# Another order for the matmuls of the down product, and another start for its rows

## The chip, the cores and the metric

The kernel runs on one core of one Trainium2 chip. The metric is the time of one execution on the device in microseconds, median of several runs. A profile is one further execution with every instruction's start and length recorded; its span runs from the first instruction to the last.

## The reference

One layer of a hybrid decoder, in float32, for 256 prompt tokens and 8 x 8 sample tokens (320 tokens, width 2048), that share the weights:

```
z = rms_norm(x) @ w_in                       # B, C, h, q, k, v and two gates
y_conv = (B * conv3(C * h)) @ w_conv_out
y_attn = window_attention(q, k, v) @ w_attn_out
h = x + (sigmoid(g_c) * y_conv + sigmoid(g_a) * y_attn) @ w_o
a = silu(rms_norm(h) @ w_gate) * (rms_norm(h) @ w_up)      # 5632 features
y = rms_norm(h + a @ w_down)
```

The change lies in the last product, `a @ w_down`, which contracts 5632 features into 2048 columns. Everything is returned in float32, with the new key, value and convolution states.

## The kernel before

**Two parts of every number.** TensorE multiplies operands of type `float32r`. Weights and activations are therefore each split into a high part, which `float32r` holds, and the small remainder, the low part. A product is the sum of three: high weight times high activation, high weight times low activation, low weight times high activation. ScalarE makes the high part of a tile of weights (`whi`, line 128), VectorE the low part (`wlo`, line 129), from a raw tile (`wraw`) that SyncE loads 512 KB at a time. The pools hold four raw tiles, three high ones and three low ones. In most products the weights are stationary, and a matmul moves the 320 columns of one part of the activations past them (`product`, line 161).

**The down product.** The 5632 features are 44 slices of 128, taken in two halves of 28 and 16 slices (`FH`). After the gate and up products of a half, `down(half, c0)` (line 930) makes 512 columns of the output at a time, that is four chunks `c` of 128 columns, one PSUM tile `ps[c]` each: four such blocks in the first half, three in the second. The last block of the second half is written out apart at the end (lines 1077 to 1116). Weights come two slices `k` at a time (a set); the last four slices of a block make one larger set. For a slice and a chunk there are up to three matmuls:

- m = 0, line 954: the high weights are stationary and 512 columns move. Of these, 320 are the high parts of all tokens and 192 the low parts of all tokens but the first 128.
- m = 1, line 958, for chunk 0 alone: the low parts of the first 128 tokens are stationary and the 512 columns of the high weights move, once for all four chunks, into a tile of its own (`dl`, or `rowacc` in the last block). This one moves weights.
- m = 2, line 962: the low weights are stationary and the 320 high columns move.

In the last block lines 1106 and 1111 are m = 0 and m = 2; there 384 columns move in m = 0, m = 1 is missing from the loop, and line 1146 brings what is left with the activations stationary and the weights moving.

**The order.** `passes(order, end)` (line 149) puts the matmuls of a set in order: m = 0 of a pair (k, c), with m = 1 behind it, then the next pair; m = 2 comes three pairs late (`LAG`). In the last set of a block, `end`, one chunk is finished before the next begins, and in the first and the last set the pairs are sorted by chunk. The chunks are sorted there because the same four PSUM tiles serve the next block: three additions on VectorE (lines 973 to 975) empty each of them into the residual.

The order of instructions on an engine is that of the text as far as the instructions' inputs are ready by the reckoning of the program that builds the kernel; it moves later work ahead of an instruction that it takes to be waiting.

**The rows.** `a_rows` (line 909) lays the activations of a half into one tile of `float32r`. Each row, 64 elements per slice and part, is read in eight streams, 4 elements from each in turn (`placed` and `turns`, lines 96 and 100). The streams lie 912 elements apart in the first half and 528 in the second; both are 16 more than a multiple of 128. `LEAD_F` elements stand ahead of the rows, and `LEAD_L` between them and the low rows of m = 1. In the program as built, a partition's high and low weights lie at byte 39040 and multiples of 4096 behind it, the activations' tile at byte 144160. Counted modulo 128 elements (512 bytes) the weights begin at 32, the rows at 112, 48 short of the weights, and the low rows of m = 1 at 32 like the weights. In the last block some of the converted weights are kept in the rest of the activations' tile (`free`), at 32 too, and some in the tile `more` at byte 96000, which is at 64, that is 32 elements further.

Of the kernel before, what the change touches and what calls it, by code (L numbers as in the profile page):

```python
# [43 lines left out]
JR = P // NP  # L44
JM = 2 * JT - JR
XB = [1] * 4 + [2] * 6
LEAD_X, LEAD_C, LEAD_A, LEAD_M, LEAD_F, LEAD_L = 16, 8, 8, 24, 40, 48
TOK = [(0, 128), (128, 128), (256, 64)]


# [1 line left out]
def hybrid_layer(ctx: ExitStack, tc: tile.TileContext, a: dict, o: list):  # L52
# [15 lines left out]
    def ps_acc(name):  # L68
        return acc.tile([P, 512], F32, tag="acc", name=name)

    def ps_aux(name):
        return aux[0].tile([P, 512], F32, tag="aux", name=name)
# [3 lines left out]
    def u(s):  # L76
        uid[0] += 1
        return f"{s}_{uid[0]}"

    def after(*marks):  # L80

        es = ExitStack()
        for m in marks:
            es.enter_context(tc.issue_after(m.ins))
        return es
# [10 lines left out]
    def placed(ap):  # L96

        return ap.rearrange("p (s j) -> p s j", s=NP)

    def turns(ap):  # L100

        return ap.rearrange("p s (i b) -> p i s b", b=4)
# [24 lines left out]
    def split_to(hi, lo, src):  # L127
        last["hi"] = nc.scalar.activation(hi, src, AF.Copy)  # L128
        last["lo"] = nc.vector.tensor_sub(lo, src, hi.bitcast(F32))  # L129
# [19 lines left out]
    def passes(order, end):  # L149

        seq, low = [], []
        for k, c in order:
            if end and low and low[-1][1] != c:
                seq, low = seq + low, []
            seq += [(k, c, 0), (k, c, 1)]
            low.append((k, c, 2))
            if len(low) > LAG:
                seq.append(low.pop(0))
        return seq + low

    def product(load, nk, xh, xl, name, tiles=None, loaded=None):

        ps = [ps_acc(u(name)) for _ in range(2)]
        k0 = 0
        for n in tiles or [min(KT, nk - k) for k in range(0, nk, KT)]:
            hi, lo = load(k0, n)
            if loaded:
                loaded()
            order = [(k, c) for k in range(n) for c in range(2)]
            if k0 + n == nk:  # L170
                order.sort(key=lambda kc: kc[1])
            for k, c, i in passes(order, k0 + n == nk):
                kc = k0 + k
                w, x = ((hi, xh), (hi, xl), (lo, xh))[i]
                last["mm"] = nc.tensor.matmul(  # L175
                    turns(fives(ps[c][:, :T])), w[:, k, c * P:(c + 1) * P], turns(x(kc)),
                    start=(kc == 0 and i == 0), stop=(kc == nk - 1 and i == 2),
                )
            k0 += n
            while pending:  # L180
                with after(last["lo"], last["mm"]):
                    pending.pop(0)()
            tick()
        return ps
# [147 lines left out]
    def kv_product(tiles, x_after):  # L332
# [4 lines left out]
        for i, n in enumerate(tiles):  # L337
            hi, lo = load_kv(k0, n)
            if i == 0:
                x_prep(1)  # L340
            for b in x_after.get(i, ()):
                x_load(b)
            order = [(k, c) for k in range(n) for c in range(4)]
            if k0 + n == KC:
                order.sort(key=lambda kc: kc[1])
            seq = passes(order, k0 + n == KC)
            if i == 0:
                seq.sort(key=lambda kcm: kcm[2])
            for k, c, m in seq:
                kc = k0 + k  # L350
                if k0 and (k, c, m) == (0, 3 if n > 1 else 1, 0) and k0 + n < KC:
                    for kk in range(tiles[i + 1]):
                        x_prep(k0 + n + kk)
                    tick()
                w, x = ((hi, xh), (hi, xl), (lo, xh))[m]
                last["mm"] = nc.tensor.matmul(  # L356
                    turns(fives(ps[c][:, :T])), w[:, k, c * P:(c + 1) * P], turns(x(kc)),
                    start=(kc == 0 and m == 0), stop=(kc == KC - 1 and m == 2),
                )
            k0 += n  # L360
            if i == 0:
                tick()
# [507 lines left out]
    for mp in range(8):  # L870
# [5 lines left out]
        for c in range(2):  # L876
            k = mp * 2 + c
# [49 lines left out]
    def h_parts(k):  # L927
        return parts_of(hT[:, k, :])

    def down(half, c0):  # L930

        nf, f0 = FH[half], half * FH[0]
        ps = [ps_acc(u("dn")) for _ in range(4)]
        low = ps_aux(u("dl")) if c0 < E0 else rowacc
        sets = [[k] for k in range(0, nf, 2)]
        sets[-2:] = [sets[-2] + sets[-1]]
        for i, k0s in enumerate(sets):
            parts = {}
            for k0 in k0s:
                raw = wp.tile([P, 2, 512], F32, tag="wraw", name=u("wraw"), bufs=4)  # L940
                nc.sync.dma_start(raw, w_d[c0 // 512, :, f0 + k0:f0 + k0 + 2, :])
                hi = wp.tile([P, 2, 512], F32R, tag="whi", name=u("whi"), bufs=3)
                lo = wp.tile([P, 2, 512], F32R, tag="wlo", name=u("wlo"), bufs=3)
                split_to(hi, lo, raw)
                for j in range(2):
                    parts[k0 + j] = (hi[:, j, :], lo[:, j, :])
            end = i == len(sets) - 1
            order = [(k, c) for k in parts for c in range(4)]
            if end or i == 0:
                order.sort(key=lambda kc: kc[1])  # L950
            for k, c, m in passes(order, end):
                cs = slice(c * P, (c + 1) * P)
                if m == 0:
                    nc.tensor.matmul(  # L954
                        turns(placed(ps[c])), parts[k][0][:, cs], turns(a_move(k)), start=k == 0, stop=False
                    )
                elif m == 1 and c == 0:
                    nc.tensor.matmul(  # L958
                        low, a_low(k), parts[k][0], start=k == 0, stop=k == nf - 1 and c0 < E0
                    )  # L960
                elif m == 2:
                    last["mm"] = nc.tensor.matmul(  # L962
                        turns(placed(ps[c])[:, :, 0:JT]), parts[k][1][:, cs], turns(a_move(k)[:, :, 0:JT]),
                        start=False, stop=k == nf - 1,
                    )
            if pending and i % 2 == 1:
                with after(last["lo"], last["mm"]):
                    pending.pop(0)()
        mark["out"] = []
        for c in range(4):  # L970
            k = c0 // P + c
            got, (first, rest) = placed(ps[c]), h_parts(k)
            nc.vector.tensor_add(first, first, got[:, :, 0:JR])
            nc.vector.tensor_add(rest, rest, got[:, :, JR:JT])
            mark["out"].append(nc.vector.tensor_add(rest, rest, got[:, :, JT:]))
        if c0 < E0:
            ys = ylow[:, c0:c0 + 512]
            if half == 0:
                nc.scalar.activation(ys, low, AF.Copy)
            else:  # L980
                nc.vector.tensor_add(ys, low, ys)

    for half in range(2):
# [86 lines left out]
        for c0 in range(0, D if half == 0 else E0, 512):  # L1070
            down(half, c0)
            if half == 1:
                pending.append(lambda c0=c0: rows_of(c0))
                pending.append(lambda c0=c0: rest_of(range(c0 // P, c0 // P + 4)))
# [23 lines left out]
    for i, ks in enumerate(sets):  # L1098
        end = i == len(sets) - 1
        order = [(k, c) for k in ks for c in range(4)]  # L1100
        if end or i == 0:
            order.sort(key=lambda kc: kc[1])
        for k, c, m in passes(order, end):
            cs = slice(c * P, (c + 1) * P)
            if m == 0:
                nc.tensor.matmul(  # L1106
                    turns(placed(ps[c])[:, :, JR:]), held[k][0][:, cs], turns(a_move(k)[:, :, JR:]),
                    start=k == 0, stop=k == nf - 1,
                )
            elif m == 2:  # L1110
                last["mm"] = nc.tensor.matmul(
                    turns(placed(ps[c])[:, :, 0:JT]), held[k][1][:, cs], turns(a_move(k)[:, :, 0:JT]),
                    start=False, stop=k == nf - 1, skip_group_check=True,
                )
        if pending and i % 2 == 1:
            with after(last["lo"], last["mm"]):
                pending.pop(0)()
# [5 lines left out]
    for c in range(4):  # L1123
        k = E0 // P + c
# [11 lines left out]
    for c in (2, 3):  # L1136
        k = E0 // P + c
# [118 lines left out]
```

## Time and profile before

| | |
|---|---|
| median of 3 runs | 1603.67 us (1603.61 to 1603.93) |
| profiled execution | 1604.88 us |
| its span | 1603.1 us |
| TensorE (PE) busy | 99% of the span |
| VectorE (DVE), ScalarE (ACT) busy | 55%, 41% |
| granted TensorE clock | 0.998 |

Busy times are of the span. In a timeline a row is a run of like instructions: start in us, length in us, engine, line, operation, tiles, shape and count. Matmuls overlap in it, since the length runs to the modelled end; what a matmul costs is the distance from its start to the next one's.

### The profile page before, as it was taken

To read this page: it belongs to the slowest core of one execution; us is meant where nothing else is said; L and a number is where in the kernel's file an instruction comes from. 1 tells how busy PE (TensorE), PEld (TensorE's weight loads), DVE (VectorE), ACT (ScalarE), POOL (GpSimd) and SP (SyncE) were. 2 spreads that over 40 slices of the span, in tenths; PEclk is the share of its full clock that TensorE was granted. 3 is DMA by queue.
4 is the path that set the end of the run, shared out by engine and by line. 5 is a ranking of instruction groups with operands and counts; after the bars stand their busy time and mean duration, and the time that the engine had idled before them with its cause. 6 is when DMAs were issued, how large, how long until landed. Compare 5 with 4: busy or idle time off the path is not lost.

```text
span 1603.1 us, 26407 instructions
## 1 busy us (share of the span) xinstructions
PE 1593.3 (99%) x10955; PEld 1555.5 (97%) x10955; DVE 885.6 (55%) x1316; ACT 651.5 (41%) x928; POOL 78.3 (5%) x123
## 2 busy tenths in 40 slices
PE   9999999999999999999999999999999999999998
PEld 9999999999999999999999999998888999999887
DVE  7879555555554445556555555553444455555556
ACT  7545343433333334444333333333333334344443
POOL 1101311000000003320000000000000000000000
PEclk9999999999999999999999999999999999999999
DMA  7554546544444444444444444444444444444552
GB/s 268 170 167 149 184 135 195 170 158 158 158 158 158 158 158 158 155 154 155 157 158 158 158 158 158 158 158 155 154 155 156 156 158 158 158 158 158 181 174 93
DMA packets 74400, 258.14 MB, mean 161 GB/s; under 512 B 8552, under 2 KB 11928, under 8 KB 74152
## 3 DMA queue, kind: packets, MB, share of 16 engines
q1 hardware_dynamic: 71880, 249.86, 47.5%
q0 software_dynamic: 1968, 5.90, 1.3%
q8 instruction: 86, 1.41, 0.4%
q10 hardware_dynamic: 432, 0.69, 0.1%
q14 instruction: 34, 0.28, 0.0%
HBM read 253.30 MB, written 5.08 MB: 161 GB/s over the span
## 4 chain that ended last, share of the span: by engine, by line
PE 98%; DVE 1%; DMA 1%; ACT 0%; issue 0%; DVEq 0%; SPq 0%; ACTq 0%
PE fu L175 18%; PE fg L175 18%; PE dn L954 9%; PE ga L175 7%; PE gc L175 7%; PE wo L175 7%; PE dn L962 6%; PE B L175 3%; PE C L175 3%; PE H L175 3%; PE ya L175 3%; PE yc L175 3%; PE q L175 3%; PE dl L958 2%; PE kv L356 1%; PE dn L1106 1%
## 5 line engine op out<-in xcount | busy, mean ns | idle before, releaser
L129 DVE TENSOR_TENSOR wlo<-wraw,whi 128x1024 fp32r<-128x1024 f32 (+1 forms) x461 | 562.1, 1220 | 590.5 <-ACT whi L128 582.1
L128 ACT ACTIVATE whi<-wraw 128x1024 fp32r<-128x1024 f32 (+1 forms) x461 | 485.6, 1055 | 718.8 <-PE dn L954 144.7
L954 PE MATMUL dn<-a_t,whi 128*128 128x512 f32 x640 | 211.0, 385 | 0.0
L175 PE MATMUL fu<-hh_t,whi 128*128 128x320 f32 x704 | 205.1, 301 | 0.0
L175 PE MATMUL fg<-hh_t,whi 128*128 128x320 f32 x704 | 205.1, 301 | 0.0
L175 PE MATMUL fu<-hl_t,whi 128*128 128x320 f32 x704 | 205.1, 301 | 0.0
L175 PE MATMUL fg<-hl_t,whi 128*128 128x320 f32 x704 | 205.1, 301 | 0.0
L175 PE MATMUL fu<-hh_t,wlo 128*128 128x320 f32 x704 | 158.8, 301 | 0.0
L175 PE MATMUL fg<-hh_t,wlo 128*128 128x320 f32 x704 | 158.8, 301 | 0.0
L962 PE MATMUL dn<-a_t,wlo 128*128 128x320 f32 x640 | 146.7, 302 | 0.0
L954 PEld LDWEIGHTS dn<-a_t,whi 128*128 128x128 f32 x640 | 118.6, 187 | 19.4
L175 PEld LDWEIGHTS fu<-hh_t,whi 128*128 128x128 f32 x704 | 131.7, 187 | 0.0
L175 PEld LDWEIGHTS fu<-hl_t,whi 128*128 128x128 f32 x704 | 131.7, 187 | 0.0
L175 PEld LDWEIGHTS fg<-hl_t,whi 128*128 128x128 f32 x704 | 131.7, 187 | 0.0
L175 PEld LDWEIGHTS fg<-hh_t,whi 128*128 128x128 f32 x704 | 131.7, 187 | 0.0
L962 PEld LDWEIGHTS dn<-a_t,wlo 128*128 128x128 f32 x640 | 111.1, 188 | 9.3
L175 PEld LDWEIGHTS fu<-hh_t,wlo 128*128 128x128 f32 x704 | 116.2, 187 | 0.0
L175 PEld LDWEIGHTS fg<-hh_t,wlo 128*128 128x128 f32 x704 | 116.2, 187 | 0.0
L175 PE MATMUL gc<-xh_t,whi 128*128 128x320 f32 x256 | 74.5, 301 | 0.0
L175 PE MATMUL gc<-xl_t,whi 128*128 128x320 f32 x256 | 74.5, 301 | 0.0
L175 PE MATMUL ga<-xh_t,whi 128*128 128x320 f32 x256 | 74.5, 301 | 0.0
L175 PE MATMUL ga<-xl_t,whi 128*128 128x320 f32 x256 | 74.5, 301 | 0.0
(309 smaller groups left out, 2676.4 us busy)
## 6 DMA issues: line engine op xcount, KB each, us to landing
wraw<-in_w_in_dram SPq DMA_DIRECT2D x128, 512.0 KB, 3.8
wraw<-in_w_gate_dram SPq DMA_DIRECT2D x88, 512.0 KB, 3.7
wraw<-in_w_up_dram SPq DMA_DIRECT2D x88, 512.0 KB, 3.6
wraw<-in_w_down_dram SPq DMA_DIRECT2D x88, 512.0 KB, 3.4
wraw<-in_w_o_dram SPq DMA_DIRECT2D x32, 512.0 KB, 3.7
wraw<-in_w_conv_out_dram SPq DMA_DIRECT2D x16, 512.0 KB, 3.6
wraw<-in_w_attn_out_dram SPq DMA_DIRECT2D x16, 512.0 KB, 3.6
wraw<-in_w_kv_dram SPq DMA_DIRECT2D x6, 512.0 KB, 6.7
```

The source lines that it names most:

```text
L128: last["hi"] = nc.scalar.activation(hi, src, AF.Copy)
L129: last["lo"] = nc.vector.tensor_sub(lo, src, hi.bitcast(F32))
L175: last["mm"] = nc.tensor.matmul(turns(fives(ps[c][:, :T])), w[:, k, c * P:(c + 1) * P], turns(x(kc)), start=(kc == 0 and i == 0), stop=(kc ...
L356: last["mm"] = nc.tensor.matmul(turns(fives(ps[c][:, :T])), w[:, k, c * P:(c + 1) * P], turns(x(kc)), start=(kc == 0 and m == 0), stop=(kc ...
L954: nc.tensor.matmul(turns(placed(ps[c])), parts[k][0][:, cs], turns(a_move(k)), start=k == 0, stop=False)
L958: nc.tensor.matmul(low, a_low(k), parts[k][0], start=k == 0, stop=k == nf - 1 and c0 < E0)
L962: last["mm"] = nc.tensor.matmul(turns(placed(ps[c])[:, :, 0:JT]), parts[k][1][:, cs], turns(a_move(k)[:, :, 0:JT]), start=False, stop=k == ...
L1106: nc.tensor.matmul(turns(placed(ps[c])[:, :, JR:]), held[k][0][:, cs], turns(a_move(k)[:, :, JR:]), start=k == 0, stop=k == nf - 1,)
```

## The change

A new function puts the matmuls of a set in turn: all m = 0 of the set (eight of them, two slices by four chunks), then m = 1 of both slices, then all eight m = 2. Where `end` is set, this is done chunk by chunk. It replaces `passes` in the down product (line 951) and in the last block (line 1103); the other products keep `passes`. `LEAD_F` goes from 40 to 52 and `LEAD_L` from 48 to 36: the rows begin 12 elements later, and the low rows of m = 1, and what lies behind them, stay where they were.

```
-LEAD_X, LEAD_C, LEAD_A, LEAD_M, LEAD_F, LEAD_L = 16, 8, 8, 24, 40, 48
+LEAD_X, LEAD_C, LEAD_A, LEAD_M, LEAD_F, LEAD_L = 16, 8, 8, 24, 52, 36
...
+    def in_turn(order, end):
+
+        groups = [[kc for kc in order if kc[1] == c] for c in range(4)] if end else [order]
+        return [(k, c, m) for g in groups for m in range(3) for k, c in g]
...
-            for k, c, m in passes(order, end):
+            for k, c, m in in_turn(order, end):
...
-        for k, c, m in passes(order, end):
+        for k, c, m in in_turn(order, end):
```

## The prediction

> **What bounds the kernel now.** I read the page first (busy shares, the chain that ended last, the costliest groups), then the busy times of the down product's stretch, then its timeline matmul by matmul.
>
> ```profile
> span 1603.1 us, 26407 instructions
> PE 1593.3 (99%) x10955; PEld 1555.5 (97%) x10955; DVE 885.6 (55%) x1316; ACT 651.5 (41%) x928; POOL 78.3 (5%) x123
> PE 98%; DVE 1%; DMA 1%; ACT 0%; issue 0%; DVEq 0%; SPq 0%; ACTq 0%
> L954 PE MATMUL dn<-a_t,whi 128*128 128x512 f32 x640 | 211.0, 385 | 0.0
> L962 PE MATMUL dn<-a_t,wlo 128*128 128x320 f32 x640 | 146.7, 302 | 0.0
> ```
>
> TensorE (PE) is busy for 99% of the span and holds 98% of the chain; the two big groups of the down product have no idle time ahead of them (the last number of their rows). Nothing that another engine or a queue does is late in this stage. The row of the first half's down product, with stretch and length, then the busy time of PE, PEld, DVE, ACT and POOL, the granted clock, the DMA share and GB/s, says the same:
>
> ```profile
> 1081.00:1269.70 188.70, 188.70 (x1011) 167.76 (x1010) 81.17 (x104) 60.93 (x62) 0.00 (x0) 1.00 0.50 156
> ```
>
> TensorE works through all 188.70 us at a granted clock of 1.00. So the change, which neither adds nor removes a matmul, can move the time in two ways only: the distance from one matmul's start to the next one's changes, or TensorE begins to wait. It touches this stretch, the second half's three blocks and the last block.
>
> One set of two slices in the first half, from its first m = 0 to that of the next:
>
> ```profile
> 1151.58 0.38 PE L954 MATMUL dn<-a_t,whi 128*128 128x512 f32 x1
> 1151.81 0.39 PE L958 MATMUL dl<-whi,a_t 128*128 128x512 f32 x1
> 1152.04 0.83 PE L954 MATMUL dn<-a_t,whi 128*128 128x512 f32 x3
> 1152.71 0.31 PE L962 MATMUL dn<-a_t,wlo 128*128 128x320 f32 x1
> 1152.85 0.38 PE L954 MATMUL dn<-a_t,whi 128*128 128x512 f32 x1
> 1153.07 0.39 PE L958 MATMUL dl<-whi,a_t 128*128 128x512 f32 x1
> 1153.31 0.30 PE L962 MATMUL dn<-a_t,wlo 128*128 128x320 f32 x1
> 1153.44 0.38 PE L954 MATMUL dn<-a_t,whi 128*128 128x512 f32 x1
> ...
> 1154.39 0.72 PE L962 MATMUL dn<-a_t,wlo 128*128 128x320 f32 x4
> 1154.94 0.38 PE L954 MATMUL dn<-a_t,whi 128*128 128x512 f32 x1
> ```
>
> A set takes 1154.94 - 1151.58 = 3.36 us. Three m = 0 in a row take 0.67, so 0.223 each; the m = 1 that moves weights 0.23 to 0.24; four m = 2 in a row 0.55, so 0.138 each. The program has 80 sets of this size: 14 in each of four blocks and 8 in each of three, with the last four slices of a block counted as two. Of these, 59 are neither first nor last in a block (11 x 4 + 5 x 3), and they alone get a really different order. The last block has eight more, with shorter matmuls.
>
> **The change part by part. The order.** In the 59 sets an m = 0 is now followed by another m = 0 seven times of eight, and an m = 2 by another m = 2. Both pairs stand in the rows of before, here in the last set of a block, where one chunk is finished after the other:
>
> ```profile
> 1125.07 1.06 PE L954 MATMUL dn<-a_t,whi 128*128 128x512 f32 x4
> 1125.97 0.73 PE L962 MATMUL dn<-a_t,wlo 128*128 128x320 f32 x4
> 1126.54 1.06 PE L954 MATMUL dn<-a_t,whi 128*128 128x512 f32 x4
> 1127.44 0.72 PE L962 MATMUL dn<-a_t,wlo 128*128 128x320 f32 x4
> 1128.01 0.38 PE L954 MATMUL dn<-a_t,whi 128*128 128x512 f32 x1
> ```
>
> Four m = 0 take 0.90 here (0.225 each) and four m = 2 take 0.57 (0.143). An m = 1 behind an m = 1 does not occur in a set of before. The nearest row is the final product, which moves weights against stationary activations 24 times in a row:
>
> ```profile
> 1590.01 5.54 PE rowacc L1146 x24
> ```
>
> That is 5.54 / 24 = 0.231 each. For the 320 columns there is also the row of the up product, whose matmuls all move 320 columns in an unbroken stream:
>
> ```profile
> 1067.61 13.44 PE fu L175 x96
> ```
>
> 0.140 each. The new set is then 8 x 0.223 + 2 x 0.231 + 8 x 0.140 = 3.366 us, against 3.36: +0.006 by 59 sets, +0.35 us. With the dearer row for both (0.225 and 0.143) it is 3.406, +0.046 a set and +2.7 us; with the cheaper (0.223 and 0.138) it is 3.350, -0.010 and -0.6 us. I take the middle, because the set keeps changing chunks, as the first row does, and the dearer row is four matmuls into one chunk. The first and the last set of a block are sorted by chunk before and after, and I cost their new order at nothing.
>
> **Where the rows begin.** No row of before has rows 12 elements further from the weights. What the trace does have is the same matmul with its weights 32 elements further: in the last block, where some weights stand in `more`. One timeline, from the first m = 0 of a set to the next set's:
>
> ```profile
> 1569.18 0.84 PE L1106 MATMUL dn<-a_t 128*128 128x384 f32 x4
> ...
> 1571.70 0.60 PE L1041 MATMUL fa<-ident,xv 128*128 128x128 f32 x4
> ...
> 1577.22 0.84 PE L1106 MATMUL dn<-a_t,more 128*128 128x384 f32 x4
> ...
> 1579.75 0.83 PE L1106 MATMUL dn<-a_t,whi 128*128 128x384 f32 x4
> ...
> 1582.24 0.84 PE L1106 MATMUL dn<-a_t,whi 128*128 128x384 f32 x4
> ```
>
> A set with its weights in line takes 2.52 us (1569.18 to 1571.70) or 2.49 (1579.75 to 1582.24), one with them in `more` 2.53 (1577.22 to 1579.75): 0.01 to 0.04 more, 0.025 against the mean. A full set moves 832 columns per pair where these move 704, so 0.025 x 832 / 704 = 0.030 a set. Twelve elements are 3/8 of the way: 0.011, by 80 sets, +0.9 us. I take this because no other row holds a shift with all else alike. The upper end is the full 0.04: 0.04 x 1.18 x 80 = +3.8 us. The lower end is below nothing, since nothing says that 48 was the best distance: within one set of before the same m = 2 takes 0.13 (1153.31 to 1153.44) or 0.14 (1152.71 to 1152.85), and an m = 0 takes 0.22 (1152.85 to 1153.07). If all matmuls came to 0.22 and 0.13, a set would be 8 x 0.22 + 2 x 0.231 + 8 x 0.13 = 3.262, 0.098 less, -7.8 us over 80 sets.
>
> Here the Trainium skill speaks against any effect: its page "SBUF — State Buffer", section "Who interferes with whom", gives TensorE two independent read ports, one for the moving operand and one for loading weights, and says that it never waits on anyone. By that rule the second part would be worth nothing and the sum +0.35. The 0.01 to 0.04 us between the sets above speak weakly against the rule.
>
> **Waits.** No DMA, conversion or queue is moved. The high weights are last read 1.12 us before a set's end (eight m = 2) instead of 0.55, which frees `whi` sooner; the low weights are first needed 2.25 us into a set instead of 1.13. Both loosen. One thing tightens: in a block's first set the fourth chunk is written after six m = 0, and its PSUM tile is still being emptied. VectorE at the same block's start:
>
> ```profile
> 1128.20 0.29 DVE L973 TENSOR_TENSOR xv<-xv,dn 128x128 f32<-128x128 f32 x1 [0.53 <-PE dn L962]
> 1128.41 0.35 DVE L974 TENSOR_TENSOR xv<-xv,dn 128x192 f32<-128x192 f32 x1
> 1128.67 1.22 DVE L129 TENSOR_TENSOR wlo<-wraw,whi 128x1024 fp32r<-128x1024 f32 x1
> 1129.81 0.35 DVE L975 TENSOR_TENSOR xv<-xv,dn 128x192 f32<-128x192 f32 x1
> ```
>
> The fourth chunk is free at 1129.81 + 0.35 = 1130.16. TensorE then:
>
> ```profile
> 1130.09 0.44 PE L962 MATMUL dn<-a_t,wlo 128*128 128x320 f32 x2
> 1130.37 0.63 PE L954 MATMUL dn<-a_t,whi 128*128 128x512 f32 x2
> ```
>
> By the written order one m = 2 stands ahead of the fourth chunk's first m = 0, and the trace has two: what builds the program has already moved ready work in front of this wait. In the new order it has two m = 1 and six or more m = 2 to put there, over 1.3 us. I cost it at nothing; that work is the cover.
>
> **The sum.** +0.35 + 0.9 = +1.25 us. The profiled execution's own time is 1604.88, its span 1603.1 and 1.78 around it; it lies 1.2 above the median of the runs, 1603.67. A difference that lies wholly inside the span applies to the median alike: 1603.67 + 1.25 = 1604.9 us.
>
> **The rivals. Reads that fall better (faster).** The new distance suits all eight streams. For it: spacings inside one set of before vary from 0.13 to 0.14 for the same work, so something costs a few per cent of a matmul here and not there. Against it: the up product runs at 0.140 for 320 columns without any variation. The bound was -7.8 us; at two thirds of it, -5, the time is 1598.7. The Trainium skill's page "TensorE: Matmul & The Clock Gate", section "Back-to-back issue gap", gives the columns over 2.4 GHz plus 2.5 ns, 0.216 and 0.136 us; an estimate by it is 10 x 0.216 + 8 x 0.136 = 3.248 a set, 9 us less in all. No row here reaches it for a whole set.
>
> **Reads that fall worse (slower).** Twelve elements cost as much as or more than 32 did, and the m = 0 in a row cost the dearer 0.225: +3.8 and +2.7, at most 1610.2; with the first alone and the likeliest order, 1607.8. For it: every other distance that the trace holds is a little slower than this one. Against it: the differences are 0.04 us a set at most.
>
> **A wait at a block's start (slower).** Left in its written order, the fourth chunk's m = 0 would stand at 1128.01 + 6 x 0.223 = 1129.35 and wait until 1130.16: 0.81 us, at the six block starts that follow another block, 4.9 us, which gives 1604.9 + 4.9 = 1609.8. Queued behind it on TensorE are the m = 1 and m = 2 of the set, which are ready. It decides from 0.54 us on (3.2 / 6). Against it stands the reordering above.
>
> **The distance makes no difference.** Then only the order counts: 1604.0.
>
> **How the numbers follow.** About 0.2%, 3.2 us, is what a measurement of this kernel can tell from no change. My forecast, 1604.9, gets 0.48, and the case without any effect of the distance 0.10; both lie within. Reads that fall better get 0.15. Reads that fall worse get 0.16, and the wait 0.11; both are beyond 3.2 us on the slow side. So faster 0.15, same 0.58, slower 0.27. The range runs from 1599.0, which takes in most of the faster case, to 1609.0, which takes in the usual size of the slower reads and leaves out their sum and the full wait.
>
> **What would show it.** In the timeline of the changed kernel: a set of the middle at 3.37 to 3.39 us, with m = 1 behind m = 1 at 0.231; no idle time ahead of line 954 or 962 as they stand there; at a block's start m = 1 and m = 2 ahead of the fourth chunk's m = 0; the sets in `more` no longer the slowest of the last block. I am wrong if a middle set is under 3.32 or over 3.41 us, or if VectorE becomes what TensorE waits for at a block's start.

## The result and the profile after

The changed kernel takes 1609.76 us, median of 6 runs (1609.05 to 1610.22), against 1603.57 for the kernel before in 6 runs (1603.08 to 1603.93): a ratio of 1.0038, 95% interval 1.0026 to 1.0051. It is 6.2 us slower, and 0.76 us beyond the range of the prediction. The profiled execution took 1610.22 us. From its page, the span, the busy shares, the chain by engine and the two groups:

```profile
span 1608.5 us, 26407 instructions
PE 1598.9 (99%) x10955; PEld 1559.8 (97%) x10955; DVE 886.3 (55%) x1316; ACT 651.6 (41%) x928; POOL 78.3 (5%) x123
PE 99%; DVE 1%; ACT 0%; issue 0%; DVEq 0%
L959 PE MATMUL dn<-a_t,whi 128*128 128x512 f32 x640 | 160.4, 387 | 0.0
L967 PE MATMUL dn<-a_t,wlo 128*128 128x320 f32 x640 | 107.3, 304 | 0.0
```

Lines have moved by five: 954 is now 959, 958 is 963, 962 is 967, 1106 is 1111. TensorE is as busy as before and waits for nobody; the smaller busy times of the groups only mean that less of their overlap is counted twice. So the same matmuls take longer. The timeline shows a middle set of the first half and the start of the next:

```profile
1138.15 1.97 PE L959 MATMUL dn<-a_t,whi 128*128 128x512 f32 x8
1139.95 0.63 PE L963 MATMUL dl<-whi,a_t 128*128 128x512 f32 x2
1140.42 1.31 PE L967 MATMUL dn<-a_t,wlo 128*128 128x320 f32 x8
1141.56 1.96 PE L959 MATMUL dn<-a_t,whi 128*128 128x512 f32 x8
```

A set takes 1141.56 - 1138.15 = 3.41 us, against 3.36; that is the highest value that the prediction still allowed. Its parts are 8 x 0.225, 2 x 0.235 and 8 x 0.143; I had put 0.223, 0.231 and 0.140. Over the seven blocks the down product takes 273.65 us instead of 270.42 (all totals of this kind are from the first m = 0 to the first matmul of what follows, summed over both halves): +3.23 us.

That is half of it. The other half stands where no instruction was changed. The chain in order of time (start, length, engine, tile, line, count) around the end of the first half, before and then after:

```profile
1269.63 13.66 PE fg L175 x96
1283.29 0.06 PE nudge L905
1283.35 13.49 PE fu L175 x96
1296.85 13.44 PE fg L175 x96
```

```profile
1271.30 13.45 PE fg L180 x96
1284.76 0.06 PE nudge L910
1284.82 13.71 PE fu L180 x96
1298.53 13.65 PE fg L180 x96
...
1476.02 13.65 PE fu L180 x96
```

These are the gate (`fg`) and up (`fu`) products of the second half, 96 matmuls of 320 columns each. Between the first two the kernel has a `nudge` (line 903), one matmul of 128 columns whose result nobody reads. A product takes 13.44 us (96 x 0.140) or 13.65 (96 x 0.142), and the products that follow keep the pace until something disturbs the stream. Before, the first runs at the slow pace and the nudge ends that. After, the first runs at the quick pace, and behind the same nudge all of them are slow: the first two products cancel out, and the 14 behind them cost 14 x 0.21 = 2.94 us. With the down product's 3.23 that is 6.2. The last block is 0.10 us quicker (20.41 against 20.51), and what stands ahead of the first gate product 0.7 us quicker in this execution, which leaves the 5.4 us between the spans.

The two paces are not the clock gate: the changed kernel's row for the slow stretch, read like the one of before, has a granted clock of 1.00.

```profile
1272.00:1490.00 218.00, 218.00 (x1536) 217.92 (x1535) 115.82 (x160) 87.62 (x128) 0.02 (x1) 1.00 0.50 156
```

### The profile page after: what moved, and what is told of

Same layout as the page of the kernel before. It is cut to its first block, busy times and chain, and to the rows that moved or that the text cites. A ratio compares the mean times of both kernels' runs of the same rounds, so it can differ in the third digit from the quotient of the medians.

```text
span 1608.5 us, 26407 instructions
## 1 busy us (share of the span) xinstructions
PE 1598.9 (99%) x10955; PEld 1559.8 (97%) x10955; DVE 886.3 (55%) x1316; ACT 651.6 (41%) x928; POOL 78.3 (5%) x123
## 4 chain that ended last, share of the span: by engine, by line
PE 99%; DVE 1%; ACT 0%; issue 0%; DVEq 0%
PE fu L180 19%; PE fg L180 18%; PE dn L959 9%; PE ga L180 7%; PE gc L180 7%; PE wo L180 7%; PE dn L967 6%; PE B L180 3%; PE C L180 3%; PE H L180 3%; PE ya L180 3%; PE yc L180 3%; PE q L180 3%; PE dl L963 2%; PE kv L361 2%; PE dn L1111 1%
## 5 line engine op out<-in xcount | busy, mean ns | idle before, releaser
L959 PE MATMUL dn<-a_t,whi 128*128 128x512 f32 x640 | 160.4, 387 | 0.0
L967 PEld LDWEIGHTS dn<-a_t,wlo 128*128 128x128 f32 x640 | 100.0, 188 | 8.6
L967 PE MATMUL dn<-a_t,wlo 128*128 128x320 f32 x640 | 107.3, 304 | 0.0
```

The lines of the kernel that those rows point to most:

```text
L959: nc.tensor.matmul(turns(placed(ps[c])), parts[k][0][:, cs], turns(a_move(k)), start=k == 0, stop=False)
L967: last["mm"] = nc.tensor.matmul(turns(placed(ps[c])[:, :, 0:JT]), parts[k][1][:, cs], turns(a_move(k)[:, :, 0:JT]), start=False, stop=k == ...
```

## The experiments

**The nudge taken out.** From both kernels the same two lines go:

```
-            if half == 1 and fpair == 0:
-                nudge()
```

> The changed kernel without the second of its two nudges (the short dummy matmul ahead of the up product of the second half's first pair). Theory A, a stream of 320-column matmuls has two states, 0.140 and 0.142 us each, and a nudge moves it from one to the other: the changed down product of the first half now leaves the stream in the quick state, so without the nudge the gate and up products of the second half stay at 13.44 us instead of 13.65, 15 products by 0.21, 3.1 us less than the changed kernel, about 1606.6 us. Rival B, the second half's products are slow for another reason (where the new rows are written, what VectorE and ScalarE do beside them): they stay at 13.65, and the time at about 1609.7 us.

> The kernel before without the same nudge. Theory A: its down product leaves the slow state (first gate product of the second half 13.66 us), nothing ends it, and the 15 products behind it stay at 13.65: 3.1 us more, about 1606.7 us. Rival B: no change, about 1603.6 us, or a state that ends by itself within a product or two.

The changed kernel without it takes 1606.27 us (ratio to before 1.0018, 1.0009 to 1.0027), 3.5 less than with it; the kernel before without it 1606.69 (1.0021, 1.0013 to 1.0030), 3.1 more. One deletion helps the one and harms the other by about the same. The chain of the changed kernel without the nudge, then of the kernel before without it:

```profile
1270.08 13.45 PE fg L180 x96
1283.53 13.44 PE fu L180 x96
1296.97 13.44 PE fg L180 x96
```

```profile
1268.32 13.65 PE fg L175 x96
1281.97 13.65 PE fu L175 x96
1295.62 13.65 PE fg L175 x96
```

Theory A stands: the pace is what the down product leaves, it lasts, and one nudge can change it either way. That the second half's products are slow for a reason of their own (B) has fallen.

**Order and start, each alone.** The changed kernel with `LEAD_F, LEAD_L` = 40, 48; then the kernel before with 52, 36.

> The new order with the rows 48 short of the weights as before. If the order costs the down product its 3.2 us (theory C: m = 0 behind m = 0 and m = 2 behind m = 2 are dearer), a middle set takes 3.41 us as in the changed kernel, and the down product with its seven blocks 273.6 us. If the new start costs it (theory D), a middle set takes 3.36 to 3.37 us and the down product about 270.5 us. In which state the second half's products run is open; 3.1 us hang on that: 1603.6 to 1604.2 or 1606.7 to 1610.

> The old order with the rows 36 short of the weights. Theory C, the order costs: middle sets at 3.36 us, the down product's seven blocks at 270.4 us. Theory D, the start costs: 3.41 us and 273.6 us. Again 3.1 us hang on the state in which the second half's products run.

The order alone takes 1604.66 us, ratio 1.0007 (0.9998 to 1.0016), so no difference that its interval shows; the start alone 1609.88, ratio 1.0042 (1.0028 to 1.0056), as much as both together. Theory C is wrong: the order costs a third of what it gave. Theory D is right of the start, but gave the order nothing. A middle set of the timeline with the order alone, and the start of the next:

```profile
1140.34 1.96 PE L959 MATMUL dn<-a_t,whi 128*128 128x512 f32 x8
1142.14 0.62 PE L963 MATMUL dl<-whi,a_t 128*128 128x512 f32 x2
1142.60 1.28 PE L967 MATMUL dn<-a_t,wlo 128*128 128x320 f32 x8
1143.72 1.96 PE L959 MATMUL dn<-a_t,whi 128*128 128x512 f32 x8
```

3.38 us a set: 8 x 0.225, 2 x 0.230, 8 x 0.140. The down product takes 271.60 us with the order alone (+1.18) and 273.76 with the start alone (+3.34). Both together give 273.65, so they do not add: with the rows 36 short the new order costs nothing. The total repeats well: in the five runs that change only nudges of the kernel before it is 270.36 to 270.49 us. And the pace goes with the start. The chain with the order alone, then with the start alone:

```profile
1269.08 13.66 PE fg L180 x96
1282.73 0.06 PE nudge L910
1282.80 13.49 PE fu L180 x96
```

```profile
1270.74 13.44 PE fg L175 x96
1284.18 0.06 PE nudge L905
1284.24 13.71 PE fu L175 x96
```

**Other starts.** The kernel before with other pairs `LEAD_F, LEAD_L` whose sum stays 88, so that only the rows move.

> The old order, rows 44 short of the weights (4 elements later than before). Down product of the kernel before 270.4 us, with 36 short 273.8. Theory R, the cost grows with the distance from 48: a third of 3.3, 271.5 us. Theory Q, every distance that is no multiple of 16 is dear alike: about 273.8 us. The state of the second half's products is whichever the new down product ends in: 3.0 us more or not.

> The old order, rows 32 short of the weights. Theory R: 16 of 12 times 3.3, about 274.8 us in the down product. Theory Q: as cheap as 48, 270.4 to 271 us. The last block's rows with 32 elements more (0.01 to 0.04 us a set) would give 271.2 to 274.2.

> The old order, rows 64 short of the weights. Theory R: about 274.8 us in the down product. Theory Q: 270.4 to 271 us.

> The old order, rows 16 short of the weights, the distance that the other products have. If that distance suits any stream read 4 elements at a time, the down product takes 270.4 us or less; if each number of streams has its own best distance, 272 to 276 us.

> The old order, rows 56 short. If cost rises smoothly on this side from 48 (270.4) to 64 (271.9): about 271.2 us. If distances off a multiple of 16 are dear, as 36 and 44 were: 273 to 276 us.

> The old order, rows 60 short. Smooth: about 271.5 us. Off a multiple of 16 dear: 273 to 276 us.

| rows short of the weights | down product, us | first gate product of the second half | products behind the nudge |
|---|---|---|---|
| 16 | 275.85 | quick | slow |
| 32 | 273.87 | quick | slow |
| 36 | 273.76 | quick | slow |
| 44 | 276.20 | slow | quick |
| 48 (before) | 270.42 | slow | quick |
| 56 | 272.43 | quick | slow |
| 60 | 273.56 | quick | slow |
| 64 | 271.88 | quick | quick |

Neither the rule of steady growth nor that of multiples of 16 holds: four elements from 48 towards the weights cost the most, 5.8 us, eight the other way 2.0, and 16 is nearly the dearest. (The rows of the gate and up products lie 16 short only if one counts modulo 64; modulo 128, as here, they lie 80 short.) 48 is the best of the eight. The runs with 44, 32 and 64 short took 1611.11, 1610.36 and 1604.51 us (ratios 1.0049, 1.0043 and 1.0007); one execution each with 16, 56 and 60 short 1612.13, 1608.92 and 1610.02.

ScalarE and VectorE, which write the next weights meanwhile, are not the cause. Taking only matmuls during which neither they nor GpSimd ran, the mean distance from one start to the next is 222.5 ns for m = 0 with 48 short and 233.0 with 44, and 137.7 and 144.6 ns for m = 2 (about 110 and 180 matmuls each). The DMA queues run in both and are not excluded by this.

**Is it the distance or the place?** Sixteen elements of padding ahead of the pool of weights and 48 behind it, and 16 more in each `LEAD` ahead of rows:

```
-LEAD_X, LEAD_C, LEAD_A, LEAD_M, LEAD_F, LEAD_L = 16, 8, 8, 24, 40, 48
+LEAD_X, LEAD_C, LEAD_A, LEAD_M, LEAD_F, LEAD_L = 32, 24, 24, 40, 56, 48
...
+    pad_t = pad_a.tile([P, 16], F32, name="pad_t")
     wp = ctx.enter_context(tc.tile_pool(name="wp", bufs=3))
...
+    pad_u = pad_b.tile([P, 48], F32, name="pad_u")
```

> The kernel before with the weights tiles 16 elements later in memory and all rows of activations 16 later with them, so the down product's rows lie where they lay in the run with 32 short, but 48 short of the weights again. If the distance between what moves and what is loaded counts: 270.4 us in the down product (32 short: 273.9), quick products, about 1603.5 us. If the place of the rows by itself counts: 273.9 us, about 1607 to 1610 us.

The down product takes 270.36 us. Its rows have moved by 80 elements in all (the padding's 64 and 16 of `LEAD_F`), the weights by 16. Modulo 64 elements the rows lie where those of 32 short lay (273.87), but the weights have come along, and the distance is 48 again. So, counted modulo 64, what matters is where the weights begin against the rows, not where the rows lie. Counted modulo 128, as in the table, the rows are 112 short, a place and a distance that no other run has; that 64 is the right count is not shown, only made likely by the agreement with 270.42. The total was a miss, 1608.96 us, because the other half of the effect struck elsewhere. In the first half there is a nudge ahead of the second pair's gate product; in the kernel before it ends a slow pace that begins behind the two matmuls of `pss2` (line 998). The chain of this run:

```profile
715.67 0.29 PE pss L202 x2
715.96 13.45 PE fu L181 x96
729.48 13.71 PE fg L181 x96
743.19 13.65 PE fu L181 x96
```

Here the pace was quick behind `pss2`, and all products of the first half behind that nudge are slow. So the last run takes it out:

> Weights and rows both 16 elements later, without the nudge of the first half. If that nudge took the stream from quick to slow, all 27 first-half products behind the first stay at 13.44 to 13.45, and with the down product at 270.4 us the time is 5.4 us under the 1608.96 of the same with the nudge: 1603.3 us, 0.3 under the kernel before at best, less than a measurement tells. If the slow state comes by itself: about 1608.9 us.

```profile
716.87 0.29 PE pss L202 x2
717.17 13.45 PE fu L181 x96
730.62 13.44 PE fg L181 x96
```

1603.29 us, 5.7 less, and against the kernel before 0.9999 (0.9990 to 1.0008): as quick as the kernel before, by another way, and no quicker that can be measured.

**What a nudge does.** The changed kernel with two in a row, the kernel before with two, three and four, and the kernel before with both nudges one product earlier:

> The changed kernel with two nudges in a row instead of one at the second half's first pair. If a nudge moves the stream from either state to the other, two put it back: the products behind stay at 13.44 and the profiled execution takes about 3 us less than the changed kernel's 1610.2, about 1607. If a nudge only ever ends in the state it ended in here, or its effect hangs on the moment: 13.65, about 1610.3.

> The kernel before with two nudges in a row at the second half's first pair, where the first one makes the stream quick. Two states and a nudge that always changes between them: slow again, 13.65 for 15 products, a profiled execution of about 1607.5 us. Three states in turn (slow, quick, quick), which the run with 64 short suggests, where a nudge left a quick stream quick: 13.44, about 1604.5 us.

> The same with three nudges. Two states: quick, about 1604.5 us. Three in turn: slow again, about 1607.5 us.

> The kernel before with four nudges where it has its second one. A cycle of four states, one slow and three quick: slow again, 13.65 for the 15 products behind, a profiled execution of about 1608 us. A state that stays quick under nudges here: 13.44, about 1605 us.

> The kernel before with both nudges one product earlier: in the first half behind the sum over partitions and ahead of the first up product, in the second half ahead of its first gate product. The products that run slow in the kernel before (the first half's first up product 13.66 us, the second half's first gate product 13.66) run at 13.44: 0.4 us less than before, about 1603.1 us. If a nudge's effect hangs on where it stands, a half or both stay at 13.65: 1606 to 1607 us or more.

In the changed kernel the second nudge takes back what the first did: one execution of 1606.72 us, and products at 13.44. In the kernel before, two, three and four all stay quick (1604.30, 1604.87 and 1604.69, one execution each; the products behind at 13.44). That is neither two states in turn nor three nor four. And with the rows 64 short, one nudge in a quick stream left it quick. With the nudges a product earlier the time is 1612.54 us (ratio 1.0057, 1.0044 to 1.0070): ahead of the first gate product, straight behind the down product, and straight behind `pss2`, the nudge does not end the slow pace. Its chain at the second place:

```profile
717.09 0.29 PE pss L196 x2
717.44 13.71 PE fu L175 x96
731.15 13.65 PE fg L175 x96
```

What the state is, and by what rule a nudge changes it, stays open. Shown is that there are two paces, that one lasts until the stream is disturbed, and that the same disturbance can end the slow one, begin it, or leave things as they are.

## Why the prediction was wrong

**Where the change acts.** "So the change ... can move the time in two ways only" was right, but the next sentence, that it touches the down product and the last block, was wrong, and it is the step that failed. It cost 2.94 us that the sum had no term for; without them the time would have been 1606.8 us, inside the range, and the changed kernel without the nudge took 1606.27. The rows were there: the chain of the kernel before has products of 13.66, 13.49 and 13.44 us, the same 96 matmuls each, and a dummy matmul between the first two. An instruction that computes nothing can set the pace of what follows; whoever changes what runs ahead of it has to price that.

**The order.** Put at +0.35, and +0.046 a set at the dear end. Measured alone, +1.18 us, 3.38 us a set. The mis-sized term is m = 0 behind m = 0: 0.225, the price of the sorted set, though the chunk changes each time, and not 0.223. m = 1 behind m = 1 (0.230 put as 0.231) and m = 2 (0.140) came out as put.

**The start.** Put at +0.9, with an upper end of +3.8; measured +3.34 alone and +2.05 under the new order (273.65 - 271.60). Drawing 3/8 of a line from the shift of 32 was without ground: the table has no line in it, and 12 elements cost as much as 16 (273.76 and 273.87). Nor was the last block a measure: it takes 20.46 to 20.60 us at all eight starts, while the down product moves by 5.8. The rival "reads that fall worse" had the mechanism and nearly the size. The rule of the Trainium skill's page "SBUF — State Buffer", section "Who interferes with whom", that TensorE has two independent read ports and never waits on anyone, was given as a case of its own, with no effect of the distance. The runs are against that case: 270.4 to 276.2 us for nothing but where the rows begin, and 270.36 again once the weights had moved along. Which read waits, and for what, they do not show.

**The faster case.** For 0.216 and 0.136 us the prediction names the Trainium skill's page "TensorE: Matmul & The Clock Gate", section "Back-to-back issue gap". That section calls its formula the gap of a single, isolated matmul and sets a stream of weight loads and matmuls apart from it, so the 9 us were no bound for this stream. No run comes near them: the cheapest down product is 270.36 us, where 9 less than before would be about 261. The range's lower end, 1599.0, also lay above this case's own 1598.7 and did not take it in as the prediction says; nothing came to hang on it.

**The waits.** Costing them at nothing was right. At a block's start in the changed kernel VectorE frees the fourth chunk at 1129.70 + 0.35 = 1130.05, and TensorE has two m = 1 and four m = 2 ahead of it (six or more m = 2 were expected), and follows without a gap:

```profile
1129.70 0.35 DVE L980 TENSOR_TENSOR xv<-xv,dn 128x192 f32<-128x192 f32 x1
```

```profile
1127.89 1.53 PE L959 MATMUL dn<-a_t,whi 128*128 128x512 f32 x6
1129.26 0.63 PE L963 MATMUL dl<-whi,a_t 128*128 128x512 f32 x2
1129.73 0.73 PE L967 MATMUL dn<-a_t,wlo 128*128 128x320 f32 x4
1130.30 0.61 PE L959 MATMUL dn<-a_t,whi 128*128 128x512 f32 x2
```

That rival's 1609.8 us is close to the measured time by luck, for a reason that did not happen.

## What to carry to other kernels

Where TensorE is never idle, the distance in memory between what it moves and the weights it loads can be a parameter of its own: scan it on the chip in small steps, since neighbours need not resemble each other (44 and 48 short lie 5.8 us apart). When the same group of instructions shows two durations in one trace, find out what switches them before changing anything ahead of it, and compare the durations of unchanged groups first when a result surprises. A dummy instruction that was tuned in is tuned to what runs before it, and has to be tried anew, with and without, after each such change.

## What was not expected of the hardware

An unbroken stream of 320-column matmuls keeps one of two paces, 0.140 or 0.142 us each, for as long as it runs (here 14 products, over 190 us), at the same granted clock of 1.00; one matmul of 128 columns or the end of another product can change which. With the same matmuls in the same order, 4 elements of distance between rows and weights (16 bytes) changed the down product from 270.42 to 276.20 us.
